# Issuing the expert stage of a decoder trunk as written, with a hand-made table for the side jobs

## The chip, the cores and the metric

The kernel runs on one core of a Trainium2 chip. The metric is the device time of one execution in microseconds (us). A span is the time from the first to the last instruction in the trace of one profiled execution.

## The reference

A decoder trunk of two layers works on one sequence of 256 tokens with a width of 1024, in float32. Layer 0 is an RWKV-7 time mix and a dense SwiGLU; layer 1 is a gated linear recurrence and a mixture of eight SwiGLU experts with a hidden width of 3584, of which each token uses two. Each sublayer has an RMS norm with shift, scale and gate. What matters here is the expert stage:

```python
logits = t @ w_router + b_router
top_v, top_i = lax.top_k(logits, 2)
comb = einsum('nk,nke->ne', softmax(top_v), one_hot(top_i, 8))
for e in range(8):
    out = out + comb[:, e, None] * swiglu(t, w_gu[e], w_d[e])
```

The weights of one expert are 44 MB in float32, and all of them are read in each execution.

## The kernel before, in words

Only the expert stage changes. It walks 56 steps `s`, that is (e, j): eight experts, each in seven groups of 512 hidden columns. Even experts are **big** (128 token slots), odd ones (`SMALL`) are **small** (64 slots). Each step reads six weight tiles of 1 MB: four of gate and up weights, two of down weights, through a ring of 13 raw tiles, by loads that stand on SP in the order of use.

For a big expert a weight tile is cut into two pieces of 128x1024. ACT casts each piece to a rounded high half (`wh`), DVE subtracts to get the low half (`wl`), and PE takes three matmuls for each product (high by high, low by high, high by low). There are five slots of `wh`/`wl`. `Stream.next` hands piece u to PE and writes down the splits up to piece u+5, so the splits of u+5 wait until PE is done with u. A big step is 12 pieces on PE: four of gate (`mg`, 24 matmuls), four of up (`mu`, 24) and four of down (`dn`, 24), where the down pieces are those of the step before (`s-1`). A small expert uses the raw tile as it is, in float32: 32 gate/up matmuls, both into `mg`, and 16 down matmuls.

Between gate/up and down of one step lie: silu of the gate on ACT (`sl`), times up on DVE (`sl`), four transposes on PE (`hp`), and a copy to `hTh` on ACT, for big experts also `hTl` on DVE. `sl`, `hTh`, `hTl` have one buffer each. The down sums stay in the two PSUM banks `dn0`, `dn1` over the seven steps.

An expert's side jobs run during its neighbours. **Gather** (for the next expert): `choice` makes a one-hot matrix `Pm` on DVE, `gather` multiplies by it on PE (`gp`), `gathered` scales and shifts on ACT. **Scatter** (of the expert before): `weigh` multiplies the down sums by the gate `gt2` on DVE (tiles that the trace calls `condr` and `cst`), `split` cuts them into `yh` (ACT) and `yl` (DVE), two matmuls `sc` on PE, an addition to `xt` on DVE; `scatter_cols` transposes `Pm` (`ptp`) into `PT`. Once, in the first expert, the order of experts is sorted (`t_rank`, `t_sel`, `t_sort`, `t_cap`, DVE) and `rows` spreads `gt2` by matmuls (`rwm`) of diagonal matrices that DVE makes.

What sets the order: every instruction of PE, ACT and DVE goes through the wrapper `InOrder` (so all have line 97 in the profile). While `on`, it pins the program order. After step 0 it is switched off, and a scheduler orders the three engines by its own costs; `order(...)` adds a few constraints that put an instruction behind a given split. Side jobs are taken from a list, `chores`, one at each piece:

```python
if s == 0:
    V.on = S.on = TE.on = False
...
prev = act(s, gps, ups, st.split)
```

Of the kernel before, what the change touches and what calls it, by code (L numbers as in the profile page):

```python
# [16 lines left out]
P = 128  # L17
D = 1024
# [325 lines left out]
def kernel_body(tc, io, out, dbg=None):  # L344
# [18 lines left out]
    with ctx:  # L363
# [1665 lines left out]
        def gu_half(e, ps):  # L2029
            xs = xg[e]  # L2030
            for q in range(4):
                chore()
                wh, wl = st.next()
                for kk in range(2):
                    k = 2 * q + kk
                    mm3(ps, xs[q][0][:, kk, :], xs[q][1][:, kk, :],
                        wh[:, kk * 512:(kk + 1) * 512], wl[:, kk * 512:(kk + 1) * 512], k == 0, k == KT - 1)

        def gu_small(e, ps):

            for h in range(2):
                w = [st.next() for _ in range(2)]
                for k4 in range(4):
                    chore()
# [4 lines left out]
        def act_small(s, ps):  # L2049
            sl = mb.tile([P, 512], F32, tag="sl", name=f"sl{s}", bufs=1)  # L2050
            S.activation(sl[HALF:P], ps[0:HALF], AF.Silu)
            V.tensor_tensor(sl[HALF:P], sl[HALF:P], ps[HALF:P], ALU.mult)
            return sl

        def tpose_small(s, hm):
            ps = pdn.tile([P, 4, HALF], F32, tag="m", name=f"hp{s}", bufs=2)
            for q in range(4):
                TE.transpose(ps[:, q, :], hm[HALF:P, q * P:(q + 1) * P], ident[HALF:P, HALF:P])
            a = mb.tile([P, 512], F32, tag="hTh", name=f"hTh{s}").rearrange("p (q c) -> p q c", q=4)[:, :, 0:HALF]
            S.copy(a, ps)  # L2060
            return a

        def act(s, gps, ups, behind):
            sl = mb.tile([P, 512], F32, tag="sl", name=f"sl{s}", bufs=1)
            a = S.activation(sl, gps, AF.Silu)
            if 0 < s < len(steps) - 1:
                order(tc, a, behind[0])
            V.tensor_tensor(sl, sl, ups, ALU.mult)
            return sl

        def tpose(s, hm, tags=("hTh", "hTl")):
            ps = pdn.tile([P, 4, P], F32, tag="m", name=f"hp{s}", bufs=2)
            for q in range(4):
                TE.transpose(ps[:, q, :], hm[:, q * P:(q + 1) * P], ident)
            a, b = (mb.tile([P, 512], F32R, tag=t, name=f"{t}{s}").rearrange("p (q c) -> p q c", q=4) for t in tags)
            S.copy(a, ps)
            V.tensor_tensor(b, ps, a.bitcast(F32), ALU.subtract)
            return a, b
# [3 lines left out]
        chores = []  # L2082
        onto_last = {}

        def chore():

            if chores:
                f = chores.pop(0)
                if f is not None:
                    f()  # L2090

        def expert_out(e):

            yg, parts = {}, {}
            if e in SMALL:
                return expert_out_small(e)

            def weigh(n):
                yg[n] = spare if n else other
                V.tensor_tensor(yg[n], dps[e][n], gt2[:, n * 512:(n + 1) * 512], ALU.mult)  # L2100

            def split(n):
# [4 lines left out]
                parts[n] = yh, yl  # L2107

            def onto(n, i):
                sl = slice(n * 512, (n + 1) * 512)  # L2110
                ps = pdn.tile([P, 512], F32, tag="m", name=f"sc{e}{n}{i}", bufs=2)
                if e == E - 1:
                    mm(ps, PTs[e][:, i, :].bitcast(F32), yg[n], True, True)
                else:
                    mm(ps, PTs[e][:, i, :], parts[n][0], True, False)
                    mm(ps, PTs[e][:, i, :], parts[n][1], False, True)
                V.scalar_tensor_tensor(xt[:, i, sl], ps, cmbq[:, i, e:e + 1], xt[:, i, sl], ALU.mult, ALU.add)

            w = [lambda n=n: weigh(n) for n in range(2)]
            p = [lambda n=n: split(n) for n in range(2)]  # L2120
            o = [lambda n=n, i=i: onto(n, i) for n in range(2) for i in range(2)]
            if e == E - 1:
                for f in w:
                    f()
                for n in range(2):
                    for i in range(2):
                        onto_last[n, i] = o[2 * n + i]
            else:
                for f in (w[0], w[1], p[0], o[0], o[1], p[1], o[2], o[3]):
                    chores.extend([f, None])  # L2130

        def expert_out_small(e):

            yg = other
            rows_ = [slice(n * HALF, (n + 1) * HALF) for n in range(2)]
            parts = []

            def weigh():
                for n in range(2):
                    V.tensor_tensor(yg[rows_[n]], dps[e][0][rows_[n]], gt2[rows_[n], n * 512:(n + 1) * 512], ALU.mult)  # L2140

            def split():
                yh = mb.tile([P, 512], F32R, tag="yh", name=f"yh{e}", bufs=1)
                yl = mb.tile([P, 512], F32R, tag="yl", name=f"yl{e}", bufs=1)
                S.copy(yh, yg)
                V.tensor_tensor(yl, yg, yh.bitcast(F32), ALU.subtract)
                parts.extend((yh, yl))

            def onto(n, i):
                sl = slice(n * 512, (n + 1) * 512)  # L2150
                ps = pdn.tile([P, 512], F32, tag="m", name=f"sc{e}{n}{i}", bufs=2)
                l = PTs[e][rows_[n], i, :]
                if e == E - 1:
                    mm(ps, l.bitcast(F32), yg[rows_[n]], True, True)
                else:
                    mm(ps, l, parts[0][rows_[n]], True, False)
                    mm(ps, l, parts[1][rows_[n]], False, True)
                V.scalar_tensor_tensor(xt[:, i, sl], ps, cmbq[:, i, e:e + 1], xt[:, i, sl], ALU.mult, ALU.add)

            o = [lambda n=n, i=i: onto(n, i) for n in range(2) for i in range(2)]  # L2160
            if e == E - 1:
                weigh()
                for n in range(2):
                    for i in range(2):
                        onto_last[n, i] = o[2 * n + i]
            else:
                for f in (weigh, split, *o):
                    chores.extend([f, None])
# [3 lines left out]
        def down_small(s, hT, qs=range(4)):  # L2172
            e, j = steps[s]
            if j == 0 and qs[0] == 0:
                dps[e] = [pdn.tile([P, 512], F32, tag="dn0", name=f"dn{e}")]
            for q in qs:
                chore()
                if q % 2 == 0:
                    wd[0] = st.next()
                for n in range(2):  # L2180
                    o = (q % 2) * D + n * 512
                    mm(dps[e][0][n * HALF:(n + 1) * HALF], hT[:, q, :], wd[0][:, o:o + 512], j == 0 and q == 0, j == NJ - 1 and q == 3)
            if j == NJ - 1 and qs[-1] == 3:
                expert_out(e)

        def down(s, hT2, qs=range(4)):
            e, j = steps[s]
            if e in SMALL:
                return down_small(s, hT2, qs)
            if j == 0 and qs[0] == 0:  # L2190
                dps[e] = [pdn.tile([P, 512], F32, tag=f"dn{n}", name=f"dn{e}{n}") for n in range(2)]
            a, b = hT2
            for q in qs:
                chore()
# [218 lines left out]
```

## Time and profile before

| | |
|---|---|
| median of 3 runs | 1530.08 us (1529.32 to 1530.34) |
| profiled execution | 1529.51 us |
| its span | 1527.7 us, mean granted PE clock 0.970 |
| PE / DVE / ACT busy | 1449.1 / 1001.2 / 752.4 us (95% / 66% / 49%) |
| chain that ended last | PE 85%, DVE 9%, ACT 3%, DMA 2% |
| expert stage | about 618 to 1516 us of the span |

In the chain, a stretch of PE alone means that nothing but PE's own work set the time; a piece of ACT or DVE in it means that PE had waited for that piece. In a timeline, square brackets hold the idle time of the engine just before the row and what ended it. Time is lost in the expert stage in two ways: PE stands still, or it runs at the lower granted clock.

### The profile page before, as it was taken

The page shows a single profiled execution, that of the slowest core. Times are in us where ns is not written, and L with a number is a line of the kernel's source. Part 1 is how long each engine was busy: PE and PEld are TensorE (multiplying, and loading weights), DVE is VectorE, ACT ScalarE, POOL GpSimd, SP SyncE. Part 2 cuts the span into 40 slices and gives each one's busy share as a digit, 9 for nine tenths or more (in the row PEclk, how much of TensorE's full clock was granted, in tenths as well). Part 3 has the DMA queues.
Part 4 walks back from the last instruction along what each step waited for, and adds up shares of the span by engine and source line. Part 5 has one row for each costly group of instructions (what it writes and reads, how often), then busy time and mean ns, then how long its engine had stood idle before and what let it go on. Part 6 is the DMA issues. An engine that isn't in the chain of part 4 may idle for free.

```text
span 1527.7 us, 20895 instructions
## 1 busy us (share of the span) xinstructions
PE 1449.1 (95%) x7847; PEld 1024.9 (67%) x7847; DVE 1001.2 (66%) x1519; ACT 752.4 (49%) x1139; POOL 52.9 (3%) x44
## 2 busy tenths in 40 slices
PE   5998898999999899999999999999999999999997
PEld 3774684999999797888543688434688434688432
DVE  7788977788887787979412788302788302788302
ACT  3667434444444675777313577213577113577101
POOL 3011700000000000000000000000000000000000
PEclk9999989999999999899999999999999999999998
DMA  9563336978888346789999999799999799999796
GB/s 370 191 234 138 111 104 266 373 291 327 337 304 322 135 163 213 265 304 369 357 390 421 421 421 369 298 387 421 421 420 370 292 393 421 421 421 362 297 418 250
DMA packets 69935, 488.54 MB, mean 320 GB/s; under 512 B 8000, under 2 KB 8384, under 8 KB 11968
## 3 DMA queue, kind: packets, MB, share of 16 engines
q1 hardware_dynamic: 69824, 487.11, 81.7%
q8 instruction: 63, 1.03, 0.3%
q14 instruction: 48, 0.39, 0.1%
HBM read 486.03 MB, written 1.05 MB: 319 GB/s over the span
## 4 chain that ended last, share of the span: by engine, by line
PE 85%; DVE 9%; ACT 3%; DMA 2%; issue 1%; SPq 0%; POOL 0%; ACTq 0%; DVEq 0%
PE mg L97 24%; PE dn L97 17%; PE fgu L97 11%; PE mu L97 10%; PE fd L97 5%; PE gp L97 2%; PE psr L97 2%; PE linx L97 2%; DVE rq L97 2%; DVE s L97 2%; PE hp L97 1%; PE u L97 1%; PE sc L97 1%; DVE wl L97 1%; DMA rq<-ada 1%; PE psk L97 1%
## 5 line engine op out<-in xcount | busy, mean ns | idle before, releaser
L97 DVE TENSOR_TENSOR wl<-rw,wh 128x1024 fp32r<-128x1024 f32 x444 | 529.0, 1220 | 93.1 <-ACT wh L97 87.4
L97 ACT CAST wh<-rw 128x1024 fp32r<-128x1024 f32 x444 | 456.4, 1051 | 164.9 <-PE fgu L97 45.0
L97 PE MATMUL mg<-rw,condr 128*64 128x512 f32 x896 | 217.7, 595 | 0.0
L97 DVE TENSOR_TENSOR sl<-sl,mg 64x512 f32<-64x512 f32 x28 | 19.4, 692 | 210.1 <-ACT sl L97 210.1
L97 PEld LDWEIGHTS mg<-rw,condr 128*64 128x64 f32 x896 | 67.0, 137 | 122.6 <-issue 120.6
L97 PE MATMUL fgu<-fxh,wh 128*128 128x256 f32 x448 | 127.4, 285 | 1.3 <-ACT fxh L97 1.3
L97 PE MATMUL fgu<-fxl,wh 128*128 128x256 f32 x448 | 127.5, 285 | 0.0
L97 PE MATMUL fgu<-fxh,wl 128*128 128x256 f32 x448 | 126.9, 283 | 0.0
L97 PE MATMUL dn<-rw,hTh 128*64 128x512 f32 x448 | 108.4, 599 | 1.0 <-ACT hTh L97 1.0
L97 ACT ACTIVATE sl<-mg 128x512 f32<-128x512 f32 (+1 forms) x56 | 33.0, 589 | 151.4 <-PE mg L97 151.3
L97 PE MATMUL mg<-wl,xh 128*128 128x512 f32 x224 | 92.4, 413 | 9.2 <-DVE wl L97 9.2
L97 PE MATMUL mg<-wh,xh 128*128 128x512 f32 x224 | 90.7, 405 | 4.9 <-ACT wh L97 4.4
L97 PE MATMUL dn<-wl,hTh 128*128 128x512 f32 x224 | 91.1, 407 | 1.0 <-DVE wl L97 1.0
L97 PE MATMUL dn<-wh,hTl 128*128 128x512 f32 x224 | 91.0, 406 | 0.0
L97 PE MATMUL mg<-wh,xl 128*128 128x512 f32 x224 | 90.2, 403 | 0.0
L97 PE MATMUL mu<-wh,xh 128*128 128x512 f32 x224 | 89.1, 398 | 0.0
L97 PE MATMUL mu<-wl,xh 128*128 128x512 f32 x224 | 88.0, 393 | 0.0
L97 PE MATMUL mu<-wh,xl 128*128 128x512 f32 x224 | 87.7, 391 | 0.0
L97 PEld LDWEIGHTS fgu<-fxh,wh 128*128 128x128 f32 x448 | 85.2, 191 | 2.1 <-ACT fxh L97 1.7
L97 PEld LDWEIGHTS fgu<-fxl,wh 128*128 128x128 f32 x448 | 85.2, 190 | 0.7 <-issue 0.5
L97 PEld LDWEIGHTS fgu<-fxh,wl 128*128 128x128 f32 x448 | 85.5, 191 | 0.2 <-issue 0.2
L97 PE MATMUL dn<-wh,hTh 128*128 128x512 f32 x224 | 81.4, 407 | 0.0
(416 smaller groups left out, 2423.9 us busy)
## 6 DMA issues: line engine op xcount, KB each, us to landing
rw<-moe_gu SPq DMA_DIRECT2D x224, 1024.0 KB, 8.0
rw<-moe_d SPq DMA_DIRECT2D x106, 1024.0 KB, 8.7
rw<-ffn_gu SPq DMA_DIRECT2D x28, 1024.0 KB, 7.5
rw<-ada SPq DMA_DIRECT2D x28, 1024.0 KB, 7.9
rq<-ada SPq DMA_DIRECT2D x19, 1024.0 KB, 5.0
rw<-ffn_d SPq DMA_DIRECT2D x14, 1024.0 KB, 6.5
rw<-lru_in SPq DMA_DIRECT2D x8, 1024.0 KB, 7.0
rw<-moe_d SPq DMA_DIRECT2D x12, 512.0 KB, 15.0
```

The costliest lines, as they stand in the source:

```text
L97: r = f(*a, **k)
```

## The change

The line that switches the wrapper off after step 0 goes, so PE, ACT and DVE keep the order in which the program writes instructions down, through all eight experts. `chores` is replaced by a table: `put(s, n, f)` enters a job and `tick(n)` runs the jobs of the present step behind piece n (0 to 7: gate/up, 8 to 11: down; in a small step 0 to 7 stand between the groups of matmuls). Transposes and `hTh` of the step before stand at ticks 1 and 2 of a big step, and at 4 of a small one. `gather` is done in four parts, not two. Loads, tiles, arithmetic and the number of instructions stay nearly the same.

```diff
-        def onehot(Pm, i, e, behind=None):
+        def onehot(Pm, i, e):
...
-            ins = V.tensor_scalar(pm, at, ps_[:, i, c:c + 1], ms_[:, i, c:c + 1], ALU.is_equal, ALU.mult)
-            if behind is not None:
-                order(tc, ins, behind)
+            V.tensor_scalar(pm, at, ps_[:, i, c:c + 1], ms_[:, i, c:c + 1], ALU.is_equal, ALU.mult)
...
-            onehot(Pms[e], i, e, st.split[1])
+            onehot(Pms[e], i, e)
...
-            if e in SMALL:
-                c += [lambda k=k: gather(e, k, 4) for k in (0, 4)]
-                c += [lambda k=k: gathered(e, k) for k in range(0, KT, 2)]
-            else:
-                for h in (0, 4):
-                    c += [lambda h=h: gather(e, h, 4)] + [lambda k=k: gathered(e, k) for k in (h, h + 2)]
-            return c
+            g = [lambda k=k: gather(e, k, 2) for k in range(0, KT, 2)]
+            d = [lambda k=k: gathered(e, k) for k in range(0, KT, 2)]
+            return c + (g + d if e in SMALL else g[:2] + d[:2] + g[2:] + d[2:])
...
             for q in range(4):
-                chore()
                 wh, wl = st.next()
...
+                tick(at + q)
...
-        def chore():
-
-            if chores:
-                f = chores.pop(0)
-                if f is not None:
-                    f()
+        plan, now = {}, [0]
+
+        def put(s, n, *fs):
+            plan.setdefault((s, n), []).extend(fs)
+
+        def tick(n):
+            for f in plan.pop((now[0], n), ()):
+                f()
...
+        put(1, 3, t_rank)
+        put(1, 6, t_sel)
...
+        put(2, 6, lambda: rows(mod(1, 5), gt2, None, pdn, "m", "m5", dgs=(other, spare), pbufs=2))
...
+        for e in range(E):
+            b = e * NJ
+            small = e in SMALL
+            if e > 0:
+                w, p, sc, add = expert_out(e - 1)
+                if small:
+                    put(b + 1, 0, w[0])
...
+                else:
+                    put(b + 1, 2, w[0])
+                    put(b + 1, 5, w[1])
+                    put(b + 2, 6, p[0])
+                    for (t, n), k in zip(((2, 10), (3, 3), (3, 10), (4, 6)), sc):
+                        put(b + t, n, sc[k])
+                        put(b + t, n + 1, add[k])
...
+            if e < E - 1:
+                c = fetch(e + 1)
+                at_ = ([(2, 5), (2, 6), (3, 1), (3, 2), (3, 5), (3, 6), (3, 8), (3, 9), (3, 10), (3, 11)] if small else
+                       [(5, 3), (5, 6), (5, 7), (5, 8), (5, 9), (5, 10), (5, 11), (6, 3), (6, 5), (6, 7)])
+                for (t, n), f in zip(at_, c, strict=True):
+                    put(b + t, n, f)
...
+            if s > 0:
+                put(s, 4 if small else 1, lambda s=s: tpose(s - 1))
+                put(s, 4 if small else 2, lambda s=s: tparts(s - 1))
...
+                put(s, 5, lambda s=s: silu(s))
+                put(s, 9, lambda s=s: times(s))
...
-            if s == 0:
-                V.on = S.on = TE.on = False
```

**Place 1: ACT, last step of small expert 5 (s = 41) and the start of big expert 6.** `wh514` to `wh521` are the casts of the first eight pieces of step 42. Before:

```order
L97 ACTIVATE sl40_10491<-mg40_10459 64x512
L97 COPY hTh40_10546<-hp40_10541 128x4x64
L97 ACTIVATE sl41_10548<-mg41_10506 64x512
L97 COPY hTh41_10615<-hp41_10610 128x4x64
L97 CAST wh514_10511<-rw334_10509 128x1024
L97 CAST wh515_10523<-rw334_10509 128x1024
L97 CAST wh516_10529<-rw335_10527 128x1024
L97 CAST wh517_10551<-rw335_10527 128x1024
```

After:

```order
L97 ACTIVATE sl40_10491<-mg40_10459 64x512
L97 CAST wh514_10511<-rw334_10509 128x1024
L97 CAST wh515_10523<-rw334_10509 128x1024
L97 CAST wh516_10529<-rw335_10527 128x1024
L97 COPY hTh40_10540<-hp40_10535 128x4x64
L97 ACTIVATE sl41_10548<-mg41_10506 64x512
L97 CAST wh517_10551<-rw335_10527 128x1024
L97 CAST wh518_10561<-rw336_10559 128x1024
L97 CAST wh519_10570<-rw336_10559 128x1024
L97 CAST wh520_10582<-rw337_10580 128x1024
L97 CAST wh521_10597<-rw337_10580 128x1024
L97 COPY hTh41_10607<-hp41_10592 128x4x64
```

The casts of the new expert moved from behind `hTh41` to three ahead of `hTh40` and five ahead of `hTh41`.

**Place 2: ACT, end of big expert 4 and start of small expert 5 (s = 34 and 35).** `wh474` to `wh477` are the casts of the down pieces of step 34. Before:

```order
L97 ACTIVATE sl34_10062<-mg34_9967 128x512
L97 CAST hTh34_10139<-hp34_10134 128x512
L97 ACTIVATE sl35_10143<-mg35_10101 64x512
L97 CAST wh474_10091<-rw296_10089 128x1024
L97 CAST wh475_10102<-rw296_10089 128x1024
L97 CAST wh476_10108<-rw297_10106 128x1024
L97 CAST wh477_10120<-rw297_10106 128x1024
```

After:

```order
L97 CAST wh474_10091<-rw296_10089 128x1024
L97 CAST wh475_10102<-rw296_10089 128x1024
L97 CAST wh476_10108<-rw297_10106 128x1024
L97 CAST wh477_10120<-rw297_10106 128x1024
L97 CAST hTh34_10133<-hp34_10128 128x512
L97 ACTIVATE sl35_10143<-mg35_10101 64x512
```

The four casts moved ahead of `hTh34` and of `sl35`, which waits for the gate/up matmuls of step 35.

**Place 3: DVE, step 33 of the changed kernel.** `wl457` is the low half of the last piece of the step, the second `Pm5` is the second one-hot for expert 5:

```order
L97 TENSOR_TENSOR wl455_9835<-rw284_9819,wh455_9834 128x1024
L97 TENSOR_TENSOR wl456_9847<-rw285_9844,wh456_9846 128x1024
L97 TENSOR_TENSOR wl457_9859<-rw285_9844,wh457_9858 128x1024
L97 TENSOR_SCALAR Pm5_9831<-cst_59,wr_2281 128x128
L97 TENSOR_TENSOR wl458_9872<-rw286_9869,wh458_9871 128x1024
```

On PE the same kernel has the first gather matmuls straight behind the last up piece, and the down pieces behind those:

```order
L97 MATMUL mu33_9833<-wl453_9806,xh43_8891 128x512
L97 MATMUL mu33_9833<-wh453_9805,xl43_8892 128x512
L97 MATMUL gp50_9881<-Pm5_9831,mhh_5616 128x64 x2
L97 MATMUL gp50_9881<-Pm5_9831,mhl_5617 128x64 x2
L97 MATMUL gp50_9881<-Pm5_9831,mhh_5616 128x64 x2
L97 MATMUL gp50_9881<-Pm5_9831,mhl_5617 128x64 x2
L97 MATMUL dn40_9267<-wh454_9821,hTh32_9815 128x512
```

Before, both one-hots stand in step 31 and all gather matmuls follow later in one group.

## Rows read from the trace of the kernel before

**Rows 1.** Waits of PE, 618 to 1516 us: us in total, times, longest.

```profile
PE mg L97 <- DVE wl L97: 9.2, 6, 2.3
PE mg L97 <- ACT wh L97: 4.4, 3, 1.5
PE hp L97 <- DVE sl L97: 4.2, 3, 1.4
PE ptp L97 <- DVE xt L97: 1.8, 3, 0.6
...
PE sc L97 <- DVE condr L97: 0.8, 1, 0.8
```

**Rows 2.** Chain that ended last, 826 to 1440 us: start, us, what.

```profile
829.28 1.89 PE dn L97 x8
...
833.88 5.60 PE mg L97 x23
...
955.28 5.56 PE dn L97 x24
...
962.43 7.02 PE mg L97 x30
...
972.45 6.47 PE dn L97 x20
...
1060.85 7.16 PE mg L97 x23
...
1282.76 1.72 PE dn L97 x8
1284.86 1.89 PE dn L97 x8
...
1289.46 7.13 PE mg L97 x23
...
1302.10 3.61 PE dn L97 x16
...
1308.44 3.04 PE mg L97 x12
...
1419.62 7.03 PE mg L97 x30
...
1429.64 6.49 PE dn L97 x20
```

**Rows 3.** Timeline of ACT, 1272 to 1310 us.

```profile
1286.83 0.37 ACT L97 COPY hTh<-hp 128x256 f32<-128x256 f32 x1 [3.41 <-PE dn L97]
1287.10 5.78 ACT L97 CAST wh<-rw 128x1024 fp32r<-128x1024 f32 x6
```

**Rows 4.** Windows: length, busy time by engine; last three: PE clock, DMA share, GB/s.

```profile
1185.00:1212.00 27.00, 25.04 (x98) 13.28 (x98) 9.61 (x12) 6.05 (x8) 0.00 (x0) 0.94 0.80 314
1275.00:1290.00 15.00, 12.76 (x61) 4.36 (x58) 2.51 (x3) 4.13 (x7) 0.00 (x0) 1.00 1.01 421
1290.00:1294.00 4.00, 4.00 (x12) 3.14 (x11) 4.00 (x5) 3.05 (x5) 0.00 (x0) 0.57 1.01 420
```

**Rows 5.** Chain that ended last, 955 to 985 us.

```profile
961.84 0.59 PE hp L97 x4
...
970.09 1.05 ACT wh L97
```

**Rows 6.** Timeline of DVE, 655 to 675 us.

```profile
659.48 1.23 DVE L97 TENSOR_TENSOR wl<-rw,wh 128x1024 fp32r<-128x1024 f32 x1 [0.17 <-ACT wh L97]
...
662.62 0.69 DVE L97 TENSOR_TENSOR condr<-vec,mods 128x512 f32<-128x512 f32 x1
...
663.83 0.34 DVE L97 TENSOR_SCALAR Pm<-cst,wr 128x128 fp32r<-128x128 f32 x1
```

**Rows 7.** Loads: timeline of SP, 1264 to 1275 us.

```profile
1265.09 7.18 SPq L176 DMA_DIRECT2D rw<-moe_gu  x4
```

**Rows 8.** Loads issued from 1264 to 1275 us: KB each, median us to landing.

```profile
rw<-moe_gu SPq DMA_DIRECT2D x4, 1024.0 KB, 16.7
```

More of the change, by code (lines that the diff above doesn't have):

```diff
@@ L2043, in gu_small @@
                 for k4 in range(4):
-                    chore()
                     k = 4 * h + k4
@@ L2063, in act @@
[L2063 to L2078, printed above, removed]
@@ L2080, in kernel_body, with silu @@
-        dps = {}
-        chores = []
-        onto_last = {}
-        def chore():
-            if chores:
-                f = chores.pop(0)
-                if f is not None:
-                    f()
+                    tick(k)
+        sl, hps, hTs = {}, {}, {}
+        def silu(s):
+            z = steps[s][0] in SMALL
+            sl[s] = mb.tile([P, 512], F32, tag="sl", name=f"sl{s}", bufs=1)
+            S.activation(sl[s][HALF:P] if z else sl[s], gus[s][0][0:HALF] if z else gus[s][0], AF.Silu)
@@ new lines, in times, with tpose @@
+        def times(s):
+            if steps[s][0] in SMALL:
+                V.tensor_tensor(sl[s][HALF:P], sl[s][HALF:P], gus[s][0][HALF:P], ALU.mult)
+            else:
+                V.tensor_tensor(sl[s], sl[s], gus[s][1], ALU.mult)
+        def tpose(s):
+            r = slice(HALF, P) if steps[s][0] in SMALL else slice(0, P)
+            hps[s] = ps = pdn.tile([P, 4, r.stop - r.start], F32, tag="m", name=f"hp{s}", bufs=2)
+            for q in range(4):
+                TE.transpose(ps[:, q, :], sl[s][r, q * P:(q + 1) * P], ident[r, r])
@@ new lines, in tparts @@
+        def tparts(s):
+            if steps[s][0] in SMALL:
+                hTs[s] = mb.tile([P, 512], F32, tag="hTh", name=f"hTh{s}").rearrange("p (q c) -> p q c", q=4)[:, :, 0:HALF]
+                S.copy(hTs[s], hps[s])
+                return
+            a, b = (mb.tile([P, 512], F32R, tag=t, name=f"{t}{s}").rearrange("p (q c) -> p q c", q=4) for t in ("hTh", "hTl"))
+            hTs[s] = a, b
+            S.copy(a, hps[s])
+            V.tensor_tensor(b, hps[s], a.bitcast(F32), ALU.subtract)
@@ L2092, in expert_out @@
+        dps = {}
+        plan, now = {}, [0]
[4 more added lines that the diff above has]
+                f()
         def expert_out(e):
-            yg, parts = {}, {}
-            if e in SMALL:
-                return expert_out_small(e)
+            yg, parts, ps = {}, {}, {}
+            small = e in SMALL
+            rows_ = [slice(n * HALF, (n + 1) * HALF) if small else slice(0, P) for n in range(2)]
@@ L2107, in split, with scatter @@
                 parts[n] = yh, yl
+                if small:
+                    parts[1] = parts[n]
+            def scatter(n, i):
+                r = rows_[n]
+                ps[n, i] = pdn.tile([P, 512], F32, tag="m", name=f"sc{e}{n}{i}", bufs=2)
+                l = PTs[e][r, i, :]
+                if e == E - 1:
+                    mm(ps[n, i], l.bitcast(F32), yg[n][r], True, True)
+                else:
+                    mm(ps[n, i], l, parts[n][0][r], True, False)
+                    mm(ps[n, i], l, parts[n][1][r], False, True)
@@ L2119, in expert_out @@
[L2119 to L2127, printed above, removed]
-            else:
-                for f in (w[0], w[1], p[0], o[0], o[1], p[1], o[2], o[3]):
-                    chores.extend([f, None])
@@ L2132, in expert_out_small @@
[L2132 to L2168, printed above, removed]
@@ L2170, in kernel_body @@
-        wd = {}
[L2172 to L2194, printed above, removed]
-                wh, wl = st.next()
-                for n in range(2):
-                    cl = slice(n * 512, (n + 1) * 512)
-                    mm(dps[e][n], a[:, q, :], wh[:, cl], j == 0 and q == 0, False)
-                    if s < len(steps) - 1:
-                        mm(dps[e][n], a[:, q, :], wl[:, cl], False, False)
-                    mm(dps[e][n], b[:, q, :], wh[:, cl], False, j == NJ - 1 and q == 3 and s < len(steps) - 1)
-                if s == len(steps) - 1:
-                    for n in range(2):
-                        mm(dps[e][n], a[:, q, :], wl[:, n * 512:(n + 1) * 512], False, q == 3)
-            if j == NJ - 1 and qs[-1] == 3:
-                expert_out(e)
@@ L2208, in kernel_body @@
-        prev = None
-        for s, (e, j) in enumerate(steps):
-            gps = pgu.tile([P, 512], F32, tag="g", name=f"mg{s}")
-            if e in SMALL:
-                gu_small(e, gps)
-            else:
-                gu_half(e, gps)
+                V.scalar_tensor_tensor(xt[:, i, sl], ps[n, i], cmbq[:, i, e:e + 1], xt[:, i, sl], ALU.mult, ALU.add)
+            return [[lambda n=n, f=f: f(n) for n in range(2)] for f in (weigh, split)] + [
+                {(n, i): (lambda n=n, i=i, f=f: f(n, i)) for n in range(2) for i in range(2)} for f in (scatter, onto)]
@@ new lines, in kernel_body, with down @@
+        wd = {}
+        def down(s, qs=range(4)):
+            e, j = steps[s]
+            small = e in SMALL
+            if j == 0 and qs[0] == 0:
+                dps[e] = [pdn.tile([P, 512], F32, tag=f"dn{n}", name=f"dn{e}{n}") for n in range(1 if small else 2)]
+            for q in qs:
+                first, last = j == 0 and q == 0, j == NJ - 1 and q == 3
+                if not small:
+                    wh, wl = st.next()
+                    for n in range(2):
+                        cl = slice(n * 512, (n + 1) * 512)
+                        mm3(dps[e][n], hTs[s][0][:, q, :], hTs[s][1][:, q, :], wh[:, cl], wl[:, cl], first, last)
+                else:
+                    if q % 2 == 0:
+                        wd[0] = st.next()
+                    for n in range(2):
+                        o = (q % 2) * D + n * 512
+                        mm(dps[e][0][n * HALF:(n + 1) * HALF], hTs[s][:, q, :], wd[0][:, o:o + 512], first, last)
+                tick(8 + q)
@@ new lines, in kernel_body @@
+        w7, _, sc7, add7 = expert_out(E - 1)
+        gus = {}
+        for s, (e, j) in enumerate(steps):
+            now[0] = s
+            small = e in SMALL
+            gus[s] = [pgu.tile([P, 512], F32, tag="g", name=f"mg{s}")]
+            if s > 0:
+                put(s, 4 if small else 1, lambda s=s: tpose(s - 1))
+                put(s, 4 if small else 2, lambda s=s: tparts(s - 1))
+            if small:
+                gu_small(e, gus[s][0])
+                silu(s)
+                times(s)
+            else:
+                put(s, 5, lambda s=s: silu(s))
+                put(s, 9, lambda s=s: times(s))
+                gu_half(e, gus[s][0], 0)
```

79 lines of the change are left out of this document (34 added, 45 removed).

## Prediction

> **What bounds the kernel now.** The chain of waits comes first: PE is 85% of it, so only time in which PE stands still or runs slowly can be won. The change touches the expert stage alone, so I read PE's waits there [rows 1]. They name few partners: the low and high halves of split weights (9.2 and 4.4 us, before gate matmuls), `sl` before a transpose (4.2), and two kinds of scatter work (1.8 and 0.8). The chain by time [rows 2] shows where.
>
> *Small to big*, three times (826, 1055 and 1284 us). PE ends the last eight small down matmuls at 1284.86 + 1.89 = 1286.75 and starts the row of 23 gate matmuls at 1289.46, a gap of 2.71; at the first place 829.28 + 1.89 = 831.17 to 833.88, also 2.71. A second gap follows one step later, 1302.10 + 3.61 = 1305.71 to 1308.44, 2.73. ACT's timeline [rows 3] gives the cause: the six casts of the new expert's pieces start only behind `hTh` of the last small step, which waits for PE (3.41 idle). ACT was idle, and the first tile had been there: its load was issued at 1265.09 [rows 7] and loads of that stretch took 16.7 us [rows 8], so it landed at about 1281.8.
>
> *Big to small*, three times (962, 1191, 1419 us). PE ends the gate/up matmuls of the first small step at 962.43 + 7.02 = 969.45, and the down matmuls of the last big step only at 972.45 + 6.47 = 978.92 [rows 2], 9.47 later; 24 such matmuls took 5.56 a step earlier. Last of the three: 1426.65 to 1436.13, 9.48. Here the casts of the down pieces stand on ACT behind `sl` of the small step, which needs all of PE's gate/up matmuls; the chain goes through the cast at 970.09 [rows 5].
>
> *The clock.* Behind such stalls the granted clock falls to its lower level of 1.2 GHz for a while: 0.57 is the mean of 1290 to 1294 [rows 4], and the 23 gate matmuls took 7.13 and 7.16 at the two later starts against 5.60 at the first one, where it stayed at 2.4 GHz [rows 2].
>
> **What the change takes away.** (1) At small to big, Place 1 shows three casts ahead of `hTh40` and five ahead of `hTh41`, so the splits run while PE still does small matmuls. Both gaps should go. One gate matmul ran inside each gap (that is why 23 remain), 5.60/23 = 0.24. So 2.71 + 2.73 - 2 x 0.24 = 4.96 at each of three starts, 14.9; with the clock at two of them (7.13 - 5.60 = 1.53, and 1.56), **18.0**. The least is 0, if the new wait of rival 1 takes it.
>
> (2) At big to small, Place 2 shows the casts ahead of `hTh34` and `sl35`. The down matmuls then follow with no stall at full clock: 9.47 - 5.56 - 0.59 (four transposes, from the row of the big step [rows 5], an upper bound, done elsewhere now) = 3.3, three times, **10.0**. The two scatter waits of rows 1 go as well, since weighing, splitting and scattering are now steps apart: 1.8 + 0.8 = **2.6**. The first such change of expert, at 740, has no stall and gives nothing. Together 30.6.
>
> **What it adds.** The wrapper makes each queue wait at its head. In a big step DVE's queue always holds low halves that wait for PE: the split of piece u+5 needs the slot that PE frees at the end of piece u. From that point pass the cast 1.05 [rows 5], 0.17 and the subtract 1.23 [rows 6], 2.45 in all. PE does one piece, six matmuls, in 5.56 x 6/24 = 1.39. A DVE job entered at tick n is ready 2.45 plus its own time after the end of piece n, and what PE may do meanwhile is what stands between.
>
> (3) One-hot, then gather (Place 3): the second `Pm` is written at tick 6, behind the low half that waits for the end of piece 6, and PE wants it after piece 7: 2.45 + 0.34 [rows 6] - 1.39 = 1.40, in each of the four big experts, **5.6**. Before there was no such wait, because all gather matmuls came later. Bounds: 0, if DVE's neighbours are found ready, and 2.8 each (11.2), if the first one-hot and `hTl` make DVE late as well. I take 1.40, since it uses nothing but rows.
>
> (4) `weigh` of a small expert's second half stands at tick 5 of the next big expert's second step and must free bank `dn0` before the first down matmul, two pieces on: 2.45 + 0.69 (a product of the same size [rows 6]) - 2.78 = 0.36, and DVE is late by the first `weigh` and `hTl` just ahead (1.38, less 0.16 regained by each of three pieces): 1.2 at most. Three times 1.0, **3.0**; bounds 1.1 and 3.6.
>
> (5) `rows` in step 2 writes the diagonals and the matmuls that read them at the same tick: PE stands for 2.45 + 0.69 = 3.1, plus what the sorting jobs three pieces earlier make DVE late (up to 1). **4.0**, once; before, the scheduler placed those diagonals so that no wait shows in rows 1. Bounds 0 and 6, the upper one with a fall of the clock.
>
> (6) Gathers in four parts instead of two: two more detours of PE for each of seven experts. The matmuls were there before, so a detour costs less than the 0.59 that four whole transposes took [rows 5]; I take a quarter, 0.15, as an estimate, **2.1**; bounds 0 and 8.3 (14 x 0.59).
>
> (7) `hTh40` now waits for the cast of the third piece, which needs the new expert's second tile. Four loads were issued over 7.18 us from 1265.09 [rows 7], so the second landed near 1265.09 + 2.3 + 16.7 = 1284.1, and `hTh` would be ready at 1284.1 + 1.05 + 0.37 [rows 3] = 1285.5, where PE wants it at 1282.76 [rows 2]: 2.7 late if nothing moves, three times. But PE comes there about 4.2 earlier by (2), and the loads should come earlier still. From 1185 to 1212 they moved 314 GB/s, from 1275 to 1290 421 [rows 4], because raw tiles are held until the late splits are done; at the full rate that stretch gives back (1 - 314/421) x 27 = 6.9 us. 2.7 - (6.9 - 4.2) = 0. I cost it at **0**, with 0 to 8 as its bounds, and it is the basis of rival 1.
>
> The remaining moves cost nothing: silu and times are entered five pieces and more ahead of their transposes; additions to `xt` are followed by no early reader; the six loads a step keep their order on SP. There only the load of the sorted expert numbers moves, to behind eight more loads, a ring of 13 tiles ahead of use. If that cover went, a late number would hold one load, and the ring would absorb it. POOL has no work here.
>
> Sum: 30.6 won, 5.6 + 3.0 + 4.0 + 2.1 = 14.7 lost, **15.9 less**. The profiled execution took 1529.5 us, 0.6 under the median, so 1513.6 on that basis and **1514 us** beside the median of 1530.1.
>
> **A rule weighed against this.** The new waits are short, none above some 4 us, and I charge no lower clock for them: at the first small-to-big start a gap of 2.71 left the clock up [rows 2], while 2.71 at the two others brought it down. The Trainium skill, page "TensorE: Matmul & The Clock Gate", section "A second HAM failure mode: psum-queue depth-cycling", says that a PE which idles briefly and often between groups of matmuls makes its clock swing between the two levels, at a cost in throughput. That speaks against a change which trades long stalls for many short ones; by it the sum would be that of rival 2. The trace has both outcomes for the same gap, so it does not decide.
>
> **Rivals.** *1, slower: the head of ACT's queue waits for a landing.* Place: (7), `hTh` of the last small step but one behind three casts. If loads are the bound there (421 GB/s, a share of 1.01 [rows 4]) and land no earlier while PE comes 4.2 earlier, the wait is 2.7 + 4.2 = 6.9, three times 20.7, with three falls of the clock (1.55 each) 25.4: 1514 + 25.4 = about **1540**. It decides from 15.9/3 = 5.3 us a place. For it: the full rate at 1275 to 1290. Against: the lost rate at 1185 to 1212.
>
> *2, the clock.* If the lower clock follows each of the eight new waits (four of (3), three of (4), one of (5)), eight times 1.55 = 12.4: about **1526**. For it: two of three starts above. Against: the waits of (3) and (4) are about half as long.
>
> *3, cover.* If DVE and ACT run far enough ahead that (3) to (6) hardly show, nearly all 30.6 stays: about **1500**. For it: each stall gives the splits time to catch up. Against: the slots bind, and being early cannot help there.
>
> *4, the gain is given back.* The loads are at 421 GB/s through most of a small expert, so stalls can come back as waits for landings, half of rival 1's size (12.7), or the waits of (3) to (5) are twice as long: **1527 to 1530**. That the change doesn't do what it says is excluded by the places shown.
>
> **How the numbers follow.** Forecast 0.56 (its own range 1508 to 1521), rival 1 0.11, rival 2 0.12, rival 3 0.12, rival 4 0.09. The range of **1500 to 1528** leaves out rival 1 and little of rivals 3 and 4. About 0.2% (3.1 us) can be told from no change: faster is the forecast with rivals 2 and 3, 0.80; same 0.09; slower 0.11.
>
> **What would show it.** In the changed profile, PE's waits for `wl`, `wh` and `sl` at the six places should be gone, ACT's timeline should show an `hTh` between casts at the end of a small expert, and the down matmuls behind a big expert should take about 5.6 for 24. New rows should be `gp` waiting for `Pm` (four of about 1.4), `dn` for `condr` (three of about 1.0) and `rwm` for `condr` (3 to 5). A wait of `dn` for `hTh` of 5 us or more at the end of small experts would mean rival 1; clock levels under 1 without long stalls, rival 2. The prediction is wrong if the six places still stall, or if PE's waits in the stage stay near the sum of rows 1.

## The result and the profile after

The changed kernel takes 1509.16 us (median of 4 runs, 1502.95 to 1514.80) against 1529.70 us before: a ratio of 0.9866, 95% interval 0.9826 to 0.9905. The profiled execution took 1509.39 us with a span of 1507.4, 20.3 less than before. The prediction was 1514, 1500 to 1528.

PE's waits in the expert stage of the changed kernel (us in total, times, longest) stand against [rows 1]:

```profile
PE dn L97 <- ACT hTh L97: 7.5, 4, 3.4
PE gp L97 <- DVE Pm L97: 5.2, 4, 1.3
PE rwm L97 <- DVE condr L97: 3.9, 1, 3.9
PE dn L97 <- DVE condr L97: 2.8, 3, 1.0
PE sc L97 <- DVE condr L97: 0.8, 1, 0.8
PE hp L97 <- DVE sl L97: 0.3, 1, 0.3
```

The waits for `wl` and `wh` (13.6 together) are gone, that for `sl` fell from 4.2 to 0.3, and those for `xt` went. Three new ones stand there with nearly the forecast sizes: `Pm` 5.2 (5.6 forecast), `rwm` 3.9 (4.0), `dn` for `condr` 2.8 (3.0). The largest is one that I had costed at nothing: down matmuls waiting for `hTh`, 7.5. The sum of the waits is 20.5 against 23.6 in all rows before: it hardly moved, and yet the span is 20 us shorter. So most of the gain lies in PE's own work, or in the clock at which PE does it. The clock has a part: from the first gate/up matmul of the stage to that of its last step, the granted clock was at its lower level of 1.2 GHz for 23.6 us in the trace before and for 13.8 us in the changed one. At half speed that is worth up to 4.9 us.

The page of the changed kernel, groups of instructions (busy us, mean ns, idle before), has a hint of the rest:

```profile
L97 DVE TENSOR_TENSOR wl<-rw,wh 128x1024 fp32r<-128x1024 f32 x444 | 534.6, 1222 | 161.7 <-ACT wh L97 157.7
L97 ACT CAST wh<-rw 128x1024 fp32r<-128x1024 f32 x444 | 464.5, 1051 | 280.3 <-PE mg L97 58.2
L97 PE MATMUL mg<-rw,condr 128*64 128x512 f32 x896 | 208.5, 598 | 0.0
```

The same page before:

```profile
L97 PE MATMUL mg<-rw,condr 128*64 128x512 f32 x896 | 217.7, 595 | 0.0
```

The gate/up matmuls of the small experts, 896 records of nearly the same mean, cover 9.2 us less time. Splits, on the other hand, cost what they did (1.05 and 1.22 us each); ACT and DVE only wait elsewhere.

Where in the stage the time went, as the time from the first gate/up matmul of one expert to that of the next in PE's timelines (the mended kernels are described below):

```
us                     before  changed  hTh early  all mends
expert 0 (big)          122.2    128.4      128.4      121.2
expert 1 (small)         92.2     88.6       87.2       87.2
expert 2 (big)          128.2    127.7      127.7      125.1
expert 3 (small)         98.8     89.8       87.2       87.2
expert 4 (big)          129.8    127.8      127.7      125.2
expert 5 (small)         98.8     93.8       87.2       87.2
expert 6 (big)          129.8    127.8      127.7      125.1
expert 7, six steps      79.0     71.6       72.1       72.1
```

Big experts gained 2 us or less, since their new waits eat what the new order wins, and expert 0 lost 6. The small experts gained 3.6 to 9.0. Experts 3 and 5 were alike before, but 3 gained 9.0 and 5 only 5.0. That difference leads to the `hTh` wait.

PE's timeline of the changed kernel at the end of small expert 5 (idle before in brackets):

```profile
1269.48 6.57 PE L97 MATMUL dn<-rw,hTh 128*64 128x512 f32 x16 [3.40 <-ACT hTh L97]
```

ACT's timeline there:

```profile
1265.62 1.99 ACT L97 CAST wh<-rw 128x1024 fp32r<-128x1024 f32 x2 [9.72 <-DMA rw<-moe_gu]
1268.11 1.04 ACT L97 CAST wh<-rw 128x1024 fp32r<-128x1024 f32 x1 [0.49 <-DMA rw<-moe_gu]
1269.06 0.37 ACT L97 COPY hTh<-hp 128x256 f32<-128x256 f32 x1
```

ACT's queue is held by a cast that waits 9.72 us for the load of the first tile, then by one that waits for the second; `hTh`, whose input had long been there, comes after both. The same rows at the ends of experts 1 and 3:

```profile
833.30 3.65 PE L97 MATMUL dn<-rw,hTh 128*64 128x512 f32 x16 [1.18 <-ACT hTh L97]
1050.85 3.65 PE L97 MATMUL dn<-rw,hTh 128*64 128x512 f32 x16 [2.35 <-ACT hTh L97]
```

At the third place, the one shown first, the sixteen down matmuls behind the wait also took 6.57 where they took 3.65 at the other two, at the lower clock of 1.2 GHz. The window around this place (last three columns: granted clock, DMA share, GB/s):

```profile
1268.00:1274.00 6.00, 4.52 (x12) 1.45 (x14) 5.34 (x5) 3.90 (x5) 0.00 (x0) 0.55 1.01 422
```

The window of the same kernel around one of the short `Pm` waits, without a fall:

```profile
1150.00:1158.00 8.00, 6.70 (x34) 5.47 (x33) 6.88 (x9) 4.77 (x6) 0.00 (x0) 1.00 1.02 420
```

### The profile page after: what moved, and what is told of

Its sections match the earlier page's. It is cut to its first block, busy times and chain, and to the rows that moved or that the text cites. A ratio compares the mean times of both kernels' runs of the same rounds, so it can differ in the third digit from the quotient of the medians.

```text
span 1507.4 us, 20933 instructions
## 1 busy us (share of the span) xinstructions
PE 1428.0 (95%) x7847; PEld 1010.2 (67%) x7847; DVE 1005.7 (67%) x1519; ACT 757.3 (50%) x1139; POOL 52.5 (3%) x44
## 3 DMA queue, kind: packets, MB, share of 16 engines
HBM read 486.03 MB, written 1.05 MB: 323 GB/s over the span
## 4 chain that ended last, share of the span: by engine, by line
PE 78%; DVE 9%; DMA 7%; ACT 3%; issue 2%; SPq 0%; POOL 0%; DVEq 0%; ACTq 0%
PE mg L97 19%; PE dn L97 16%; PE fgu L97 11%; PE mu L97 7%; PE fd L97 5%; DMA rw<-moe_gu 5%; DVE wl L97 3%; PE gp L97 2%; PE psr L97 2%; PE linx L97 2%; DMA rq<-ada 2%; PE v L97 2%; PE u L97 2%; DVE rq L97 1%; PE hp L97 1%
## 5 line engine op out<-in xcount | busy, mean ns | idle before, releaser
L97 DVE TENSOR_TENSOR wl<-rw,wh 128x1024 fp32r<-128x1024 f32 x444 | 534.6, 1222 | 161.7 <-ACT wh L97 157.7
L97 ACT CAST wh<-rw 128x1024 fp32r<-128x1024 f32 x444 | 464.5, 1051 | 280.3 <-PE mg L97 58.2
L97 PE MATMUL mg<-rw,condr 128*64 128x512 f32 x896 | 208.5, 598 | 0.0
L97 PEld LDWEIGHTS mg<-rw,condr 128*64 128x64 f32 x896 | 59.7, 136 | 107.0 <-issue 102.5
L97 PE MATMUL dn<-wh,hTh 128*128 128x512 f32 x224 | 91.3, 408 | 2.8 <-DVE condr L97 2.8
L97 ACT COPY hTh<-hp 128x256 f32<-128x256 f32 x28 | 10.4, 371 | 158.4 <-PE hp L97 154.9
L97 PE MATMUL mg<-wl,xh 128*128 128x512 f32 x224 | 88.5, 395 | 0.0
## 6 DMA issues: line engine op xcount, KB each, us to landing
rw<-moe_d SPq DMA_DIRECT2D x12, 512.0 KB, 14.9
```

Of the source, the lines that this page charges most:

```text
L97: r = f(*a, **k)
```

## The experiments

Ten kernels ran. Each is compared with the kernel before on the same chip (1529.8 to 1531.1 us in the three sets) and, by its times, with the changed kernel's 1509.2.

### hTh early

The transposes and `hTh` of the last small step but one are written ahead of the first `st.next` of the last small step, so ahead of the new expert's casts:

```diff
-            if s > 0:
+            if small and j == NJ - 1:
+                tpose(s - 1)
+                tparts(s - 1)
+            elif s > 0:
```

> The changed kernel, with the transposes and the hTh copy of the last small step but one written down at the start of the last small step, ahead of the first cast of the new big expert. Theory A (the head of ACT's queue): in the changed kernel PE's down matmuls wait 6.9 us in all at the three ends of small experts for hTh, which stands behind three casts that wait for a landing, and once the clock falls (some 2.9 us more). These waits go and nothing takes their place: 7 to 10 us faster than the changed kernel's 1509, about 1500 to 1502, and runs closer together than 1503 to 1515. Theory B (loads are the bound there): PE comes to the new expert earlier and waits for its splits or landings instead; within 2 us of 1509.

1495.9 us (1495.5 to 1498.3), ratio 0.9780 (0.9764 to 0.9797): 13.3 less than the changed kernel, more than forecast. The wait is down to 0.5 in PE's waits:

```profile
PE dn L97 <- ACT hTh L97: 0.5, 1, 0.5
```

ACT's timeline of this kernel shows that casts still wait for the same landings, with nobody behind them that PE needs:

```profile
1259.47 1.99 ACT L97 CAST wh<-rw 128x1024 fp32r<-128x1024 f32 x2 [5.97 <-DMA rw<-moe_gu]
1261.96 1.04 ACT L97 CAST wh<-rw 128x1024 fp32r<-128x1024 f32 x1 [0.50 <-DMA rw<-moe_gu]
1263.03 0.59 ACT L97 ACTIVATE sl<-mg 64x512 f32<-64x512 f32 x1
```

In the table, experts 1, 3 and 5 are now all 87.2. The expert stage, first to last step, is 10.2 us shorter in the two profiled executions; the other 3.3 lie outside it, where start and tail of the profiled executions differ by that much between kernels that are alike there. Theory A holds. The spread fell from 11.9 to 2.8 us: it may be that the runs of the changed kernel differed by how late those landings were, but that is not shown.

### Which engine's order matters

Four kernels set the order by program or by scheduler. First the changed kernel with its table, all three engines left to the scheduler after step 0:

```diff
                 plan.pop((0, 9))
+                V.on = S.on = TE.on = False
```

> The changed kernel with its table, but with the wrapper switched off after step 0 as before, so that the scheduler orders the three engines. Theory A (the order of the casts and of the pairs of small matmuls makes the gain, the table only keeps the side jobs out of the way): the casts of a new expert stand behind hTh again and pairs are broken again, PE's waits for wh, wl and sl return (about 18 us), and the waits for Pm, condr and rwm mostly go: 1522 to 1532. Theory B (the table makes the gain): stays within 4 us of 1509.

1531.2 us (10 runs), ratio 1.0008 (0.9999 to 1.0018): nothing is left of the gain. PE's waits, the first three:

```profile
PE mg L97 <- ACT wh L97: 9.3, 6, 1.6
PE mg L97 <- DVE wl L97: 5.9, 12, 0.8
PE hp L97 <- DVE sl L97: 4.3, 3, 1.4
```

They are those of [rows 1] again, and ten pairs of small matmuls are broken (what that means and costs follows below). The table is worth nothing without the order. Then the opposite, the kernel before with its list of chores, wrapper left on:

```diff
-            if s == 0:
-                V.on = S.on = TE.on = False
             if s == 1:
```

> The kernel before with its list of chores, but with the wrapper left on after step 0: program order alone, no table. Theory A: its casts stand ahead of hTh and sl as in the changed kernel, so the waits for wh, wl and sl at the six places are gone and no pair of small matmuls is broken; the side jobs of the list, one at each piece, make a few more waits behind splits than the table does: 1508 to 1518. Theory B (the table makes the gain): the chores stall PE behind the splits, 1525 or slower.

1515.1 us, ratio 0.9900 (0.9883 to 0.9916): program order alone gives 15 of the 20 us. It has new waits of its own, since the old text writes transposes at the end of each step and the diagonals straight ahead of `rwm`:

```profile
PE dn L97 <- ACT hTh L97: 13.4, 25, 0.7
PE rwm L97 <- DVE condr L97: 5.9, 1, 5.9
```

Theory A holds, and the table is worth the other 6.

Then the changed kernel with PE in program order, ACT and DVE by the scheduler (`V.on = S.on = False`):

> The changed kernel with its table, PE in program order, but ACT and DVE ordered by the scheduler. Beside the run with all three left to the scheduler (1531.2 us) this tells what PE's order is worth: ten pairs of small matmuls that it broke are whole again (0.85 to 1.0 us each), and the casts of a new expert stand behind the sl of the last small step, no longer behind its hTh. Theory A (broken pairs and late casts share the loss): 1512 to 1522, with PE's waits for wh and wl smaller than there but not gone. Theory B (all of the loss is late splits on ACT and DVE): 1526 or slower.

1498.9 us, ratio 0.9793 (0.9777 to 0.9810): far below both forecasts, and 10 faster than the change itself. With ACT and DVE in program order and PE by the scheduler (`TE.on = False`):

> The changed kernel with its table, ACT and DVE in program order, but PE ordered by the scheduler. The casts stand as in the change, and thirteen pairs are broken. Theory A: no wait of PE for wh or wl at the start of big experts; the breaks cost 11 to 13 us, of which up to 10 are hidden because PE then waits less for hTh behind landings: 1510 to 1520. Theory B (PE's order is worth nothing): 1503 to 1509.

1503.9 us, ratio 0.9826 (0.9810 to 0.9842), within theory B's numbers, though its reason (PE's order is worth nothing) is refuted by the run before: PE's order alone takes 1531.2 to 1498.9. Its largest wait is a new one, for `gathered` on ACT (its tile `condr`):

```profile
PE gp L97 <- ACT condr L97: 3.1, 2, 1.5
```

PE's waits with PE in order and the two others free:

```profile
PE mg L97 <- DVE wl L97: 7.6, 7, 2.3
PE sc L97 <- DVE condr L97: 0.8, 1, 0.8
PE dn L97 <- ACT hTh L97: 0.5, 1, 0.5
```

The scheduler, once PE's order is given, puts `Pm`, `condr` and `hTh` ahead of splits, so none of the change's new waits is there; some late splits remain. My two theories took the losses as if they added up over the engines. They do not: with either side fixed, the scheduler arranges the other around it. Why it places PE's `hp` and side jobs, and ACT's casts, against each other when all three are free was not looked into.

### Broken pairs

A small expert's gate/up matmuls come in pairs that fill the two column halves of PE. In float32 each matmul stands as two records, a pair as four; the 32 gate/up matmuls and 16 down matmuls named for a small step above are records, 16 and 8 matmuls in the kernel's text. PE's timeline of the kernel before, behind the last down matmuls of expert 4:

```profile
1207.92 1.07 PE L97 MATMUL mg<-rw,condr 128*64 128x512 f32 x2
1208.96 0.49 PE L97 MATMUL sc<-yh,PT 128*128 128x512 f32 x1
1209.69 0.50 PE L97 MATMUL sc<-yl,PT 128*128 128x512 f32 x1 [0.23 <-DVE yl L97]
1210.12 3.65 PE L97 MATMUL mg<-rw,condr 128*64 128x512 f32 x14
1213.69 0.50 PE L97 MATMUL sc<-yh,PT 128*128 128x512 f32 x1
```

The changed kernel at the same place:

```profile
1195.72 3.65 PE L97 MATMUL mg<-rw,condr 128*64 128x512 f32 x16
1199.30 0.50 PE L97 MATMUL sc<-yh,PT 128*128 128x512 f32 x1
1199.64 0.40 PE L97 MATMUL sc<-yl,PT 128*128 128x512 f32 x1
1199.96 1.08 PE L97 MATMUL mg<-rw,condr 128*64 128x512 f32 x4
```

Fourteen records take as long as sixteen, and two take as long as four: half a pair costs a whole one. The scheduler had slipped side jobs between the halves. Sixteen times in the kernel before, two records stand by themselves like this, and the run that follows is two short of a multiple of four; in the changed kernel every run divides by four. The 9.2 us of busy time above understate it, going by the rows: each run adds its own end (four records 1.08, sixteen 3.65, so about 0.2 a run), and the changed kernel has 72 runs where there were 55. To price a break, the side jobs of small gate/up stretches were written between the halves:

```diff
                         mm(ps[z * HALF:(z + 1) * HALF], xsm[:, k, :], ...)
-                    tick(k)
+                        if z == 0:
+                            tick(k)
```

> The changed kernel, with the side jobs of small experts' gate/up stretches written between the two matmuls of a pair (which fill the two column halves) instead of behind the pair; nothing else moves. About 45 jobs with work on PE are hit. Theory A (a pair that is broken cannot overlap; the scheduler before had broken 16, and 9.2 us of busy time of these matmuls went with the change): 0.6 to 0.9 us a job, 27 to 40 us slower than the changed kernel, 1536 to 1549. Theory B (the fall of that busy time has another cause, such as the clock): within 3 us of 1509.

1511.1 us, ratio 0.9877 (0.9860 to 0.9893): theory B by its number. But the steps of its trace are longer where a stretch is broken, 13.51 to 14.37, 14.15 to 14.99 and 15.60 to 16.44 us, in eleven steps 9.3 together. Of that, 6.8 came back in the last steps of small experts: waits of `dn` for `hTh` fell from 7.5 to 1.3, and the clock at the third end stayed up (1.00 from 1262 to 1274 us).

```profile
PE dn L97 <- ACT hTh L97: 1.3, 2, 0.8
```

So a delay ahead of a wait for a landing was mostly taken up by that wait. Also, halves left over pair up with the next ones, so not each job costs, but each odd stretch. The rows below are from the run that follows: fourteen records take as long as sixteen, but the four behind the two side jobs, the second half of one pair and the first of the next among them, take what a pair takes.

```profile
1196.98 3.65 PE L97 MATMUL mg<-rw,condr 128*64 128x512 f32 x14
1200.56 0.50 PE L97 MATMUL sc<-yh,PT 128*128 128x512 f32 x1
1200.89 0.40 PE L97 MATMUL sc<-yl,PT 128*128 128x512 f32 x1
1201.22 1.08 PE L97 MATMUL mg<-rw,condr 128*64 128x512 f32 x4
```

The same edit was made once more on the kernel with `hTh` early, which has no such wait:

> The kernel with hTh written down early (1495.9 us), and with the side jobs of small experts' gate/up stretches between the two matmuls of a pair. Theory A: a break leaves one matmul alone at the start or the end of a stretch, 0.85 us each as the steps of the earlier pair run showed (13.51 to 14.37, 14.15 to 14.99, 15.60 to 16.44); in that run it was hidden, since PE then waited less for hTh behind landings. With that wait gone it shows: about 3 a small expert and one more in each ordinary small step, 10 to 20 us, so 1505 to 1516. Theory B: breaks are free even so, 1494 to 1498.

1510.0 us, ratio 0.9861 (0.9845 to 0.9878): 14.1 more than 1495.9. Theory A. The expert stage is 14.2 longer in the profile; 15 steps are 0.84 to 0.86 us longer, 12.7 together, the rest is one step of big expert 6, in which the lower clock followed a `Pm` wait of 1.33. The window of this kernel there:

```profile
1375.00:1385.00 10.00, 10.00 (x54) 8.73 (x54) 4.43 (x5) 3.14 (x3) 0.00 (x0) 0.83 1.01 416
```

### The three forecast waits

Each on top of `hTh` early. The second one-hot two pieces earlier:

```diff
-                       [(5, 3), (5, 6), (5, 7), (5, 8), ...
+                       [(5, 3), (5, 4), (5, 7), (5, 8), ...
```

> The kernel with hTh written down early (1495.9 us), and with the second one-hot of a small expert at tick 4 instead of 6, three pieces ahead of the gather. Theory A (PE waits for Pm because it stands behind a low half that waits for PE): the four waits of 1.3 us go, 5.2 us in all, 1490 to 1492. Theory B (DVE is late in any case, or what is won is waited for again at a landing): 1494 or more, with the waits still there or moved to splits.

1490.6 us (1486.6 to 1492.5), ratio 0.9729 (0.9710 to 0.9747), 5.3 less than 1495.9. No wait for `Pm` is left, and the four steps with a gather went from 22.1 to 20.7, 1.4 each, as worked out in (3).

The diagonals of step 2 ahead of their matmuls:

```diff
-        put(2, 6, lambda: rows(mod(1, 5), gt2, ...))
+        put(2, 3, lambda: diag(0), lambda: diag(1))
+        put(2, 7, lambda: spread(0), lambda: spread(1))
```

> The kernel with hTh written down early (1495.9 us), and with the two diagonals of step 2 at tick 3 and their matmuls at tick 7, instead of both at 6. Theory A: the wait of 3.9 us before rwm goes and with it the stretch of lower clock behind it (up to 1.5 us): 1490 to 1492. Theory B: the diagonals make DVE late for the splits of step 2 and the wait moves there: 1494 or more.

1490.8 us, ratio 0.9732 (0.9715 to 0.9748), 5.1 less. Step 2 went from 24.47 to 18.77, 5.7. PE's timeline of the changed kernel:

```profile
664.60 2.05 PE L97 MATMUL rwm<-condr,ones 128*128 128x512 f32 x2 [3.89 <-DVE condr L97]
666.43 1.71 PE L97 MATMUL rwm<-cst,ones 128*128 128x512 f32 x2
```

The same rows of the mended kernel:

```profile
660.37 1.02 PE L97 MATMUL rwm<-condr,ones 128*128 128x512 f32 x2
661.23 1.02 PE L97 MATMUL rwm<-cst,ones 128*128 128x512 f32 x2
```

Behind the wait they ran at the lower clock; that is the part above 3.9.

All mends, with the second `weigh` at tick 3 instead of 5 as well:

> All mends together: hTh early, second one-hot at tick 4, second weigh of a small expert at tick 3 instead of 5, diagonals at tick 3 and their matmuls at 7. Theory A (each of these waits is on the path and the loads have room: 84 tiles at 2.49 us are 209 us, and a big and a small expert now take 215): 1495.9 less 5.2, 2.8, 3.9 and up to 1.5 for the clock, 1482 to 1484. Theory B (landings take over): 1488 or more, with PE or ACT waiting for loads.

**1482.15 us** (1480.16 to 1483.34), ratio 0.9675 (0.9659 to 0.9691), 27 less than the changed kernel and the fastest version here. The steps with the second `weigh` went from 18.3 to 17.2, 1.15 each. PE's waits in the stage are down to these:

```profile
PE sc L97 <- DVE condr L97: 0.8, 1, 0.8
PE dn L97 <- ACT hTh L97: 0.5, 1, 0.5
PE hp L97 <- DVE sl L97: 0.3, 1, 0.3
```

Its windows (of big experts 4 and 6) tell how much room is left: PE is busy throughout at the full clock, and the loads run at 421 GB/s.

```profile
1040.00:1165.00 125.00, 125.00 (x567) 98.24 (x566) 107.48 (x104) 92.31 (x105) 0.00 (x0) 1.00 1.01 421
...
1255.00:1380.00 125.00, 125.00 (x569) 97.08 (x569) 107.19 (x103) 90.69 (x104) 0.00 (x0) 1.00 1.01 421
```

A pair of experts takes 212.4 us, and its 84 tiles of 1.05 MB take 209 at that rate. A further gain on PE would have to be 3 us a pair or less, or the loads take over.

## Why the prediction was right, point by point

The sign, the range and three of the new waits were right. That the size came so near (15.9 less forecast, 20.5 measured) is luck in part: two errors of opposite sign, one of 13.6 and one of 9.8.

- **(1), small to big, 18.0.** Right: no wait for `wl` or `wh` is left at the three starts. The waits that went are 13.6, where I had 14.9 beside the clock. But part of it was taken back by (7), as the range for it had allowed.
- **(2), big to small, 10.0 and 2.6.** At the first small steps the waits went (`sl` 4.2 to 0.3, `dn` for `wl` 1.0 to none); the rest of the 10.0 is the lower clock behind them, at which 20 down matmuls took 6.47 where 24 took 5.56 a step earlier. Of the 2.6, the 1.8 of `ptp` for `xt` went, but the 0.8 of `sc` for `condr` stayed: it is one wait in the scatter of the last expert, which the change leaves as it was. I had misread that row; `sc` for `yl`, 0.7, went instead. I put the stall on ACT's order alone. It also goes with ACT left to the scheduler and PE in program order, and the other way round, so the stall needs both of the scheduler's orders: ACT's casts behind `sl`, and PE's `hp` ahead of the big expert's down matmuls. What failed here is a term that is absent: I took PE's own work as fixed and only its waits as movable. **Sixteen broken pairs**, at the 0.85 us that the pair run gives, are 13.6 us that went too (worked out from that price, not measured in the kernel before itself). The rows that show them, two records in 1.07 us, were in the trace before.
- **(3), 5.6; (4), 3.0; (5), 4.0.** Measured as waits: 5.2, 2.8, 3.9. Removed, they gave 5.3, three times 1.15 (steps of the run with all mends; no run has it alone), and 5.1. The rule behind them, that a job of tick n is ready 2.45 us plus its own time after PE ends piece n, holds to a tenth for `Pm`. In (5) the lower clock was only in my upper bound and was really there.
- **(6), 2.1.** No run separates it. The gather matmuls themselves cost no more: PE is busy with them for 29.67 us before and 29.64 after. What the detours cost the matmuls beside them stays open.
- **(7), 0.** This step failed. The waits were 1.18, 2.35 and 3.40, together 6.9, and 2.9 of lower clock behind the third; the bound was 8 without the clock. I had the loads come 6.9 earlier and PE only 4.2. At the third place PE wanted `hTh` at 1269.48 - 3.40 = 1266.08, which is 83.9 us behind the expert's first gate/up matmul (1182.21); before it was 93.4 (1282.76 in [rows 2], less 1189.40). So PE came 9.5 earlier, and the five pairs that had been broken in this expert are 4.3 of that. The cast of the second tile began at 1268.11, 85.9 behind the same matmul, against 94.7 for the 1284.1 that I had worked out: 8.8 earlier. The loads won more than I had said, PE more still, and 2.7 + 9.5 - 8.8 is the 3.40 of the row. It was the mechanism of rival 1, at two fifths of its price (9.8 against 25.4).

Together: 15.9 forecast, 13.6 more from pairs, 9.8 less by (7), gives 19.7; the span fell by 20.3. That they meet so closely is chance in part. From the first gate/up matmul of the stage to that of its last step the time fell by 23.3 (878.8 to 855.5), and 3.0 of it was lost ahead of and behind that stretch, where each end differs by up to 2.4 us between kernels that are alike there. Read from the two traces, PE's idle time in the stretch fell by 3.1 (22.3 to 19.2) and the clock gave up to 4.9; with 13.6 for the pairs that makes 21.6, and 1.7 stays open.

The rivals: 1 is there in kind, at 1.18, 2.35 and, with the clock, 6.3 us a place; together 9.8, below the 15.9 (three times 5.3) from which it decides. 2 did not come: the window with a `Pm` wait of 1.3 has a clock of 1.00, and after the first step of the stage the lower level showed only behind the waits of 3.40 and 3.9. The rule of the Trainium skill that a PE which idles briefly and often has its clock swing ("TensorE: Matmul & The Clock Gate", section "A second HAM failure mode: psum-queue depth-cycling") is hardly seen in the changed kernel: of its waits of 0.9 to 2.35 none was followed by the lower level. But other traces here have the fall behind waits as short: the kernel before behind all three of its waits of 1.41 with one of 0.32 (0.66 from 972 to 977 us), the kernel with PE left to the scheduler behind both of its `gp` waits of 1.53 (0.50 from 1003 to 1006 and from 1225 to 1228), the second pair run behind one of its four of 1.3 (window above). So it came out right to charge no lower clock for the waits of (3) and (4), but not because they are short: the length of a wait alone does not tell, and what does stays open. 3 is refuted by the waits, and 4 by the time.

What holds `hTh` is what the Trainium skill states in "PSUM — Partial Sum Buffer", section "Engine vs sequencer instructions": the queue of ScalarE is strictly first in, first out. The trace agrees, with an `hTh` of 0.37 us standing behind a cast that waited 9.72. For the pairs, the Trainium skill's page "TensorEngine Tiling (Array Packing)", section "Key Properties", says that separate tiles of PE work in parallel; the trace agrees: a pair takes 1.08 us, where one half alone takes 1.07.

## What to carry to other kernels

When an order is fixed by hand, ask for each instruction what stands ahead of it and what that waits for: a job behind a split that waits for PE is ready a fixed time later, and a job behind one that waits for a load is as late as the load. Write what PE needs soon ahead of what waits long. Before counting waits, compare the busy time of equal groups of matmuls too, since an order that breaks pairs costs time that no view of waits shows; and price such a cost on a kernel without a wait behind it that would hide it. Do not add up effects that were measured one engine at a time: the order fixed on PE alone gave 1498.9, on ACT and DVE alone 1503.9, on all three 1509.2.

## What was not expected of the hardware

- Half of a column pair alone takes as long as the pair, so a break costs 0.84 to 0.86 us for a matmul of this shape (two records of 128x512 in float32), and a left-over half pairs up again with the next.
- The steps repeat to within 0.1 us from kernel to kernel where nothing differs (11.36, 15.60 and 10.84 us in all that share them), so one step's change can be read off directly, far below what a time of the whole kernel tells.
